# Four of a decode head's six early value loads placed one by one along the round trip of the attention weights, tied to products

## The chip, the cores and the metric

The kernel runs on one core of one Trainium2 chip. Times are microseconds of device time for one execution. Before the change three runs gave 2443.78, 2444.54 and 2450.01; the median is 2444.54.

## The reference

The kernel computes one step of a layer with two kinds of attention heads, for 1024 frames of a new stream (the prompt) and for 16 new frames of each of 8 running streams (the sample, or decode, side), whose keys and values of 1024 earlier frames lie in two caches. Width is 2048, there are 8 stick-breaking heads and 8 retention heads of 128. Cut to what matters here:

```python
def stick_breaking_block(q, k, v, q_start):
    z = jnp.einsum('bqhd,bkhd->bhqk', q, k) * (HEAD_DIM ** -0.5)
    strict = (k_pos[None, :] < q_pos[:, None])[None, None]
    log_beta = jax.nn.log_sigmoid(z)
    log_keep = jnp.where(strict, jax.nn.log_sigmoid(-z), 0.0)
    later = lax.cumsum(log_keep, axis=3, reverse=True) - log_keep
    a = jnp.where(strict, jnp.exp(log_beta + later), 0.0)
    return jnp.einsum('bhqk,bkhd->bqhd', a, v)

    # sample side, in reference()
    q_sb, k_sb, v_sb, gate_sb, q_r, k_r, v_r, gate_r = project(h, w_in[l], pos_s)
    k_all = jnp.concatenate([cache_sb_k[l], k_sb], axis=1)
    v_all = jnp.concatenate([cache_sb_v[l], v_sb], axis=1)
    o_sb = stick_breaking_block(q_sb, k_all, v_all, past)
```

`project` is one multiplication of the normalised input by `w_in` (2048 x 8192); both kinds of heads are normalised, gated, concatenated and multiplied by `w_out`. Everything is float32.

## The kernel before, in words

**Stages.** The prompt's 8 row tiles of 128 and the sample's one tile are worked in two groups: group 0 is tiles 0 to 3 and the sample tile (640 columns), from about 20 to 1270 us of the profile, and group 1 is tiles 4 to 7 (to about 2000 us). In each group a loop runs over the 8 heads, some 140 us each in group 0. The output projection follows. The change touches group 0 alone, because only that group has a decode side.

**The projections, which are most of TensorE's work.** `project` (L226 holds its products) takes a block of 128 columns of `w_in` in four chunks. Each chunk is a load of 256 KB on the SP queue (`wr`, L212), which ScalarE copies to its high part `wh` (L129) and VectorE turns into the rest `wl` (L130); TensorE then does 24 products of it: `wh` with the high and the low part of the input, and `wl` with the high part. `wr`, `wh` and `wl` have four buffers each, so that a load goes out when the chunk four earlier has been split. `project_rows` (L285) does the same for the values of two heads at a time, with the names `wrn`, `whn` and `wln`.

**The attention beside them.** Everything else of a head is written as Python generators, called jobs. After each product (or pair of products) of a projection `tick()` lets at most one job take a step, and the number that a job yields says how many ticks later it wants to go on. So the text order of the program is made by these numbers (`D_ZC`, `D_TO`, `D_TI`, ...), which differ for group 0 and group 1. The tile framework then orders each engine's instructions; `tied(ins)` (L151) tells it, in group 0 only, that `ins` must not come ahead of the last product written so far. This is a matter of order; no semaphore is set or waited for.

**A decode head** (`decode`, from L622), in order of its steps:

- Its cached keys come in 16 loads (`kc`, POOL queue, L642 and after), are transposed by VectorE (`kcT`, L680) and multiplied with the queries (`zc`, L658), eight key loads at a time.
- `load_v(k)` loads 512 KB of cached values (`vc`, L686, SP queue). There are eight such loads. Six of them (`V_BUFS`) are issued in one list comprehension, L692 before the change, as soon as the second half of the keys has been multiplied.
- The scores of the new keys (`zn`) follow, then the weights: sigmoids, masks on POOL, a product scan on VectorE (`weights`).
- **The round trip.** The weights `be` are written to DRAM (`turn_out`, tensor `s_bd`), and 32 ticks later (`D_TO[0]`) read back turned, in four transfers on the SP queue (`turn_in`, L478); another 32 ticks later (`D_TI[0]`) VectorE transposes them in blocks of 32 into `kp`.
- **The products with the values** `pd` (L719), two value loads at a time, 18 ticks apart. As soon as the products with values 0 and 1 are written, values 6 and 7 are loaded; VectorE copies the result (`do`, L726 and L728).

The `kcT` tiles and the `vc` tiles share one set of six buffers. A head uses eight tiles of the one and eight of the other: `vc` 0 and 1 take the buffers of the first half of the keys, `vc` 2 to 5 wait for the products `zc` of the second half, and `vc` 6 and 7 wait for the products `pd` with values 0 and 1.

**Other names that come up.** `kb` is a tile with the weights of the prompt's stick-breaking heads: they too make a round trip through DRAM, but on the POOL queue (its reads are also at L478), are transposed at L575 and multiplied at L615 (`pa`). `ro` and `so` are the outputs of the retention and the stick-breaking heads, which make a round trip of the same kind on the SP queue (L478) for the last normalisation and gating (`sg`, L549). `rs`, `sc`, `pS`, `rkn`, `S` belong to the retention heads. SP also issues the loads `dT` and `st`.

Each engine, and SP as the issuer of its queue, works its own list in order: an instruction that waits holds up what stands behind it in that list.

Of the kernel before, what the change touches and what calls it, by code (L numbers as in the profile page):

```python
# [43 lines left out]
V_BUFS = 6  # L44
D_RET = (9, 5)
D_TO = (32, 23)
D_TA = (14, 0)
D_TB = (17, 33)
D_TI = (32, 13)
# [9 lines left out]
def tile_hybrid_step(  # L59
# [26 lines left out]
    nc = tc.nc  # L86
# [61 lines left out]
    phase = [0]  # L148
    anchor = [None]

    def tied(ins):  # L151

        if phase[0] == 0 and anchor[0] is not None:
            tc.add_manual_dep(
                ins.ins,
                anchor[0].ins.name,
                mybir.DependencyInfo(mybir.DependencyClass.NoSync, mybir.DependencyReason.SCHED_ONLY),
                reason="tied to the products",
            )
# [139 lines left out]
    with ExitStack() as s1:  # L299
# [168 lines left out]
        def turn_out(src, tag, q=nc.scalar):  # L468

            s = scr.tile([src.shape[1], P, P], F32, name=tag)  # L470
            q.dma_start(s.rearrange("k q c -> q k c"), src)
            return s

        def turn_in(s, raw, q):

            for i in range(4):
                tied(
                    q.dma_start(  # L478
                        raw[32 * i : 32 * i + 32, :].rearrange("p (k a) -> p k a", a=32),
                        s[:, :, 32 * i : 32 * i + 32].rearrange("k (j b) a -> b (k j) a", b=32),  # L480
                    )
                )
# [139 lines left out]
        def decode(h, qs, rest):  # L622
# [10 lines left out]
            def chunk(m):  # L633
                s, r = divmod(m, NB)
                j, c = divmod(r, 4)
                return s, j, c
# [14 lines left out]
            for m in range(-KC_AHEAD, 2 * NB + 1):  # L651
                if m > 0 and m % NB == 0:
                    s, _, _ = chunk(m - NB)
# [29 lines left out]
                    loaded.append(load(m + KC_AHEAD))  # L683
            def load_v(k):
                vc = ip.tile([P, NB, P], F32, name="vc", tag="kv", bufs=V_BUFS)
                nc.sync.dma_start(  # L686
                    vc, cache_v[0, :, k * P : (k + 1) * P, h, :].rearrange("b p d -> p b d")
                )
                return vc


            values = [load_v(k) for k in range(V_BUFS)]  # L692
            while "kT" not in rest:
                yield 3
            z = score_tile("zn")
# [3 lines left out]
            yield D_ROW  # L699
            at = kp[:, :n].rearrange("p (k q) -> p k q", q=P)  # L700
            turned = turn_out(be.rearrange("p (k c) -> p k c", c=P), f"s_bd{h}")
            yield D_TO[phase[0]]
            turn_in(turned, be, nc.sync)
            yield D_TI[phase[0]]
            tied(nc.vector.transpose(kp[:, :n], be))
            yield D_TR[phase[0]]
            while "vn" not in rest:
# [5 lines left out]
            for k0 in range(0, 8, 2):  # L713
                yield 2 * D_VC
                for k in (k0, k0 + 1):
                    vc = values.pop(0)
                    for c in range(4):
                        r = slice(32 * c, 32 * c + 32)
                        nc.tensor.matmul(  # L719
                            po[r, : 2 * P], at[:, k, r], vc[:, 2 * c : 2 * c + 2, :], start=(k == 0), stop=(k == 7)  # L720
                        )
                for k in (k0, k0 + 1):
                    if k + V_BUFS < 8:
                        values.append(load_v(k + V_BUFS))
# [161 lines left out]
        for gi, g in enumerate(GROUPS):  # L886
# [7 lines left out]
            for h in range(H):  # L894
# [29 lines left out]
                if SAMPLE in tiles:  # L924
                    drain(sub)
                    sub = Job(decode(h, qs, rest), D_DEC)
# [239 lines left out]
```

## Time and profile before

| | |
|---|---|
| median of three runs | 2444.54 us |
| the profiled execution | 2447.93 us, its span 2446.2 us |
| mean granted TensorE clock of it | 0.982 of full speed |
| TensorE (PE) busy | 2351.9 us, 96% of the span |
| VectorE (DVE) | 1257.4 us, 51% |
| ScalarE (ACT) | 915.6 us, 37% |
| GpSimd (POOL) | 648.2 us, 26% |
| DMA | 418.67 MB, 171 GB/s over the span |
| value loads `vc` | 64 of 512 KB, median 9.5 us from issue to landing |
| weight loads `wr` | 384 of 256 KB, median 4.1 us from issue to landing |

All durations in the text are of the profiled execution. Its page gives the busy time of each engine, the groups of instructions by line (L719 is line 719 of the kernel before), what ended an engine's idle time, and the median time from the issue of a DMA to its landing. `x4` at a row's end means that four like instructions follow one another and are shown as one row. In the lists of waits a row like "PE pa L615 <- DVE kb L575: 31.2, 8, 6.3" reads: TensorE's products `pa` at L615 waited for VectorE's instruction on `kb` at L575, 31.2 us in all, in eight waits, the longest of 6.3. A row of windows has the window's ends and length, the busy time of PE, PEld (weight load into the array), DVE, ACT and POOL with the number of instructions, the granted clock, and the DMA engines' share with GB/s. The lines after L689 are two, four or six higher in the changed kernel: L719 becomes L725, L726 becomes L732, L728 becomes L734.

### The profile page before, as it was taken

How to read it: one execution, taken by the hardware profiler on the slowest of the kernel's cores; microseconds unless marked ns; L12 is line 12 of the kernel's file. 1: busy time of each engine (PE TensorE's matmuls, PEld its weight loads, DVE VectorE, ACT ScalarE, POOL GpSimd, SP SyncE). 2: the span in 40 equal slices, each digit the busy share in tenths (PEclk: the TensorE clock that was granted, in tenths of full speed). 3: DMA queues.
4: the chain of work that ended last, by engine and by line, in shares of the span. 5: the costliest groups of instructions: out<-in, count | busy, mean ns of one | idle time of the engine just before them, and what ended most of it. 6: DMA issues, size and time to landing. Idle time of an engine off the chain costs nothing.

```text
span 2446.2 us, 40473 instructions
## 1 busy us (share of the span) xinstructions
PE 2351.9 (96%) x14832; PEld 2114.5 (86%) x14832; DVE 1257.4 (51%) x2434; ACT 915.6 (37%) x1929; POOL 648.2 (26%) x1029
## 2 busy tenths in 40 slices
PE   7999998999999999999999999999999998999998
PEld 7998898989999898988778888898888876778787
DVE  7245444445455444446555554555555564564544
ACT  6332333333333332333333343333333443444333
POOL 3144353434445243334302111130220221000000
PEclk9999999999999999999999999999999998999999
DMA  7669779696969879698965565566556565676554
GB/s 239 170 129 212 150 175 179 160 203 148 195 151 208 162 170 186 150 214 189 205 157 158 145 144 155 140 156 148 146 148 152 148 169 150 223 220 188 186 182 133
DMA packets 674888, 418.67 MB, mean 171 GB/s; under 512 B 224512, under 2 KB 619776, under 8 KB 672256
## 3 DMA queue, kind: packets, MB, share of 16 engines
q1 hardware_dynamic: 524272, 285.99, 48.2%
q0 software_dynamic: 32256, 71.36, 13.2%
q10 hardware_dynamic: 118160, 58.74, 8.7%
q8 instruction: 116, 1.90, 0.3%
q14 instruction: 84, 0.69, 0.1%
HBM read 336.24 MB, written 79.69 MB: 170 GB/s over the span
## 4 chain that ended last, share of the span: by engine, by line
PE 77%; DMA 12%; DVE 4%; issue 3%; POOL 2%; ACT 2%; ACTq 0%; SPq 0%; DVEq 0%; POOLq 0%
PE acc L226 40%; PE accn L285 16%; PE a L987 4%; PE a L988 4%; PE a L986 3%; DMA mr<-s_y 3%; DMA wr<-w_in 3%; PE pa L615 3%; PE z L585 2%; DMA kb<-s_be 2%; DMA kc<-cache_sb_k 1%; PE pd L719 1%; DMA mr<-s_h 1%; POOL kc L642 1%; PE zc L658 1%
## 5 line engine op out<-in xcount | busy, mean ns | idle before, releaser
L226 PE MATMUL acc<-mh,wh 128*128 128x256 f32 (+2 forms) x2304 | 666.2, 342 | 3.0 <-ACT wh L129 3.0
L226 PE MATMUL acc<-ml,wh 128*128 128x384 f32 (+2 forms) x2304 | 668.2, 343 | 0.0
L226 PE MATMUL acc<-mh,wl 128*128 128x256 f32 (+2 forms) x2304 | 663.3, 341 | 0.1
L130 DVE TENSOR_TENSOR wl<-wr,wh 128x512 fp32r<-128x512 f32 (+1 forms) x576 | 392.7, 687 | 513.2 <-ACT wh L129 505.4
L129 ACT ACTIVATE wh<-wr 128x512 fp32r<-128x512 f32 (+1 forms) x576 | 356.9, 624 | 716.1 <-PE acc L226 317.8
L226 PEld LDWEIGHTS acc<-mh,wh 128*128 128x128 f32 x2304 | 424.3, 190 | 38.8 <-issue 5.8
L226 PEld LDWEIGHTS acc<-mh,wl 128*128 128x128 f32 x2304 | 428.2, 190 | 30.7 <-issue 3.3
L226 PEld LDWEIGHTS acc<-ml,wh 128*128 128x128 f32 x2304 | 426.5, 190 | 32.4 <-issue 4.9
L642 POOL DMA_DIRECT2D kc<-cache_sb_k x512 | 331.5, 653 | 373.6 <-DVE kcT L680 223.2
L285 PE MATMUL accn<-whn,mh 128*128 128x256 f32 x1152 | 330.0, 287 | 1.7 <-DVE rg L312 1.7
L285 PE MATMUL accn<-wln,mh 128*128 128x256 f32 x1152 | 326.7, 284 | 2.1 <-DVE wln L130 2.1
L285 PE MATMUL accn<-whn,ml 128*128 128x256 f32 x1152 | 326.6, 284 | 0.0
L285 PEld LDWEIGHTS accn<-whn,mh 128*128 128x128 f32 x1152 | 221.5, 193 | 11.4 <-issue 7.7
L987 PE MATMUL a<-wl,mh 128*128 128x512 f32 (+1 forms) x576 | 221.1, 384 | 7.6 <-DVE wl L130 7.6
L285 PEld LDWEIGHTS accn<-wln,mh 128*128 128x128 f32 x1152 | 221.8, 193 | 2.7 <-DVE wln L130 2.3
L285 PEld LDWEIGHTS accn<-whn,ml 128*128 128x128 f32 x1152 | 221.8, 193 | 0.0
L988 PE MATMUL a<-wh,ml 128*128 128x512 f32 (+1 forms) x576 | 220.1, 382 | 0.0
L986 PE MATMUL a<-wh,mh 128*128 128x512 f32 (+1 forms) x576 | 219.0, 382 | 0.7 <-DVE so L618 0.5
L130 DVE TENSOR_TENSOR wln<-wrn,whn 128x512 fp32r<-128x512 f32 x128 | 86.9, 686 | 100.3 <-ACT whn L129 100.2
L987 PEld LDWEIGHTS a<-wl,mh 128*128 128x128 f32 x576 | 109.0, 189 | 30.9 <-DVE wl L130 10.2
L129 ACT ACTIVATE whn<-wrn 128x512 fp32r<-128x512 f32 x128 | 79.9, 632 | 132.9 <-PE acc L226 54.4
L503 POOL TENSOR_SCALAR_AFFINE_SELECT kp<-kp 128x128 f32<-128x128 f32 x40 | 14.5, 363 | 429.7 <-ACT kp L497 429.6
(189 smaller groups left out, 2708.8 us busy)
## 6 DMA issues: line engine op xcount, KB each, us to landing
wr<-w_in SPq DMA_DIRECT2D x384, 256.0 KB, 4.1
wr<-w_out SPq DMA_DIRECT2D x184, 256.0 KB, 3.6
wrn<-w_in SPq DMA_DIRECT2D x128, 256.0 KB, 3.3
kc<-cache_sb_k POOLq DMA_DIRECT2D x512, 64.0 KB, 4.9
vc<-cache_sb_v SPq DMA_DIRECT2D x64, 512.0 KB, 9.5
xt<-x_prompt SPq DMA_DIRECT2D x8, 1024.0 KB, 5.8
xr<-x_prompt SPq DMA_DIRECT2D x8, 1024.0 KB, 6.5
out<-out ACTq DMA_DIRECT2D x12, 512.0 KB, 2.8
```

The lines of the kernel that those rows point to most:

```text
L129: nc.scalar.activation(hi, src, AF.Copy)
L130: nc.vector.tensor_tensor(lo, src, hi.bitcast(F32), ALU.subtract)
L226: last = nc.tensor.matmul(a[:, :m], lhs[:, j, :], rhs[w][:, j, o : o + m], start=(w == 0 and j == 0 and n == 0), stop=(w == KT // WQ - 1 a ...
L285: anchor[0] = nc.tensor.matmul(a, lhs[q][:, jj, ts], rhs[:, j, :], start=(w == 0 and j == 0 and n == 0 and t % 2 == 0), stop=(w == KT // 2 ...
L585: nc.tensor.matmul(z[:, :c], q2[a][:, i * P : (i + 1) * P], k2[b][:, s : s + c], start=(m == 0), stop=(m == 2),)
L615: nc.tensor.matmul(po[:, :P], at[:, j, :], vn[:, j, :], start=(j == 0), stop=(j == t))
L642: nc.gpsimd.dma_start(kc[32 * i : 32 * i + 32, :].rearrange("p (k d) -> p k d", d=32), cache_k[0, 2 * c + j, s * 512 : (s + 1) * 512, h, 3 ...
L658: mm = nc.tensor.matmul(z[r, :], qp[:, j, r], ready[2 * j + c // 2][:, c % 2, :], start=(j == 0), stop=(j == 1),)
L719: nc.tensor.matmul(po[r, : 2 * P], at[:, k, r], vc[:, 2 * c : 2 * c + 2, :], start=(k == 0), stop=(k == 7))
L986: nc.tensor.matmul(a[:, :width], hi[q][:, j, ts], wh, start=(k == 0), stop=False)
L987: nc.tensor.matmul(a[:, :width], hi[q][:, j, ts], wl, start=False, stop=False)
L988: nc.tensor.matmul(a[:, :width], lo[q][:, j, ts], wh, start=False, stop=(k == KT - 1))
```

## The change

`decode` issues the first two value loads where all six were issued. Loads 2 and 3 go into the pause between writing the weights `be` out and reading them back, one at its start and one 16 ticks later; loads 4 and 5 go into the pause between reading back and transposing, likewise. These four are passed to `tied`, so that the framework does not move them ahead of the products written before them. Loads 6 and 7 stay where they were. The number of instructions, the buffers and the transfers are the same.

```diff
             def load_v(k):
                 vc = ip.tile([P, NB, P], F32, name="vc", tag="kv", bufs=V_BUFS)
-                nc.sync.dma_start(
+                ld = nc.sync.dma_start(
                     vc, cache_v[0, :, k * P : (k + 1) * P, h, :].rearrange("b p d -> p b d")
                 )
+                if 2 <= k < V_BUFS:
+                    tied(ld)
                 return vc
 
 
-            values = [load_v(k) for k in range(V_BUFS)]
+            values = [load_v(k) for k in range(2)]
             while "kT" not in rest:
                 yield 3
...
             turned = turn_out(be.rearrange("p (k c) -> p k c", c=P), f"s_bd{h}")
-            yield D_TO[phase[0]]
+            for _ in range(2):
+                values.append(load_v(len(values)))
+                yield D_TO[phase[0]] // 2
             turn_in(turned, be, nc.sync)
-            yield D_TI[phase[0]]
+            for _ in range(V_BUFS - 4):
+                values.append(load_v(len(values)))
+                yield D_TI[phase[0]] // 2
             tied(nc.vector.transpose(kp[:, :n], be))
```

Since the program's text order and the framework decide each engine's list together, the lists show more than the diff. First SP's list in head 5, from the head's first value loads on. `vc` are value loads, `wr` weight chunks, `be` the four reads of the turned weights; before:

```order
L686 DMA vc<-cache_sb_v 128x8x128 x2
L212 DMA wr<-w_in 128x4x128 x2
L686 DMA vc<-cache_sb_v 128x8x128 x4
L212 DMA wr<-w_in 128x4x128 x4
L478 DMA be<-s_bd_10460 32x36x32 x4
L212 DMA wr<-w_in 128x4x128 x5
L686 DMA vc<-cache_sb_v 128x8x128 x2
L478 DMA ro<-s_rk_6_10693 32x20x32 x4
L478 DMA so<-s_o_5_4_0_10719 32x16x32 x4
L212 DMA wr<-w_in 128x4x128 x2
```

And after the change:

```order
L686 DMA vc<-cache_sb_v 128x8x128 x2
L212 DMA wr<-w_in 128x4x128 x4
L686 DMA vc<-cache_sb_v 128x8x128
L212 DMA wr<-w_in 128x4x128
L686 DMA vc<-cache_sb_v 128x8x128
L212 DMA wr<-w_in 128x4x128 x2
L478 DMA be<-s_bd_10452 32x36x32 x4
L686 DMA vc<-cache_sb_v 128x8x128 x2
L212 DMA wr<-w_in 128x4x128 x2
L686 DMA vc<-cache_sb_v 128x8x128 x2
L478 DMA ro<-s_rk_6_10693 32x20x32 x4
L478 DMA so<-s_o_5_4_0_10719 32x16x32 x4
```

Of the weight loads, two more now stand between the first two value loads and the third; between `be` and values 6 and 7, where five stood, there are two, behind values 4 and 5; the other three follow behind the reads of `ro` and `so`, ahead of the two that stood there.

Second, VectorE's list in head 5 from the copy of the decode result (`do`) on; before:

```order
L726 COPY do<-pd 128x128
L492 MEMSET kp 128x1
L728 SCALAR_TENSOR_TENSOR do<-pd,dec,do 128x128
L747 TENSOR_TENSOR sc<-rs,dT 128x128
L548 STREAM_TRANSPOSE kT<-so 128x512
L728 SCALAR_TENSOR_TENSOR do<-pd,dec,do 128x128
L549 SCALAR_TENSOR_TENSOR sg<-kT,gains,sg 128x512
L766 COPY ro<-pa 128x128
L137 TENSOR_SCALAR ov<-ssq_9457 128x1
L130 TENSOR_TENSOR wl<-wr,wh 128x512
```

And after:

```order
L732 COPY do<-pd 128x128
L492 MEMSET kp 128x1
L734 SCALAR_TENSOR_TENSOR do<-pd,dec,do 128x128
L753 TENSOR_TENSOR sc<-rs,dT 128x128
L548 STREAM_TRANSPOSE kT<-so 128x512
L734 SCALAR_TENSOR_TENSOR do<-pd,dec,do 128x128
L549 SCALAR_TENSOR_TENSOR sg<-kT,gains,sg 128x512
L772 COPY ro<-pa 128x128
L137 TENSOR_SCALAR ov<-ssq_9457 128x1
L130 TENSOR_TENSOR wl<-wr,wh 128x512
L787 COPY S<-pS 128x128
L130 TENSOR_TENSOR wl<-wr,wh 128x512
```

Three `wl` that stood ahead of the first of these rows now stand behind them: the `wl` shown is that of an earlier chunk than the one shown before.

Third, TensorE's list in head 5 behind the last products with values; before, a chunk's products with `wh` come in pairs of the high and the low part of the input (`mh`, `ml`) and are followed by those with `wl`:

```order
L226 MATMUL acc_10844<-mh_147,wh 128x256
L226 MATMUL acc_10845<-mh_147,wh 128x384
L226 MATMUL acc_10844<-ml_148,wh 128x256
L226 MATMUL acc_10845<-ml_148,wh 128x384
L226 MATMUL acc_10844<-mh_147,wl 128x256
L226 MATMUL acc_10845<-mh_147,wl 128x384
```

And after:

```order
L784 MATMUL pS<-rv,rkn 128x128
L751 MATMUL rs<-rq,rk 128x128
L226 MATMUL acc_10844<-mh_147,wh 128x256
L226 MATMUL acc_10845<-mh_147,wh 128x384
L226 MATMUL acc_10844<-ml_148,wh 128x256
L226 MATMUL acc_10845<-ml_148,wh 128x384
L769 MATMUL pa<-rv,sc 128x128
L226 MATMUL acc_11037<-mh_141,wh 128x256
L226 MATMUL acc_11038<-mh_141,wh 128x384
L226 MATMUL acc_11037<-ml_142,wh 128x256
L226 MATMUL acc_11038<-ml_142,wh 128x384
L226 MATMUL acc_10844<-mh_147,wl 128x256
```

Products that need only `wh`, four of them of the next projection (`acc_11037`, `acc_11038`), now stand ahead of the first one that needs `wl`.

## The prediction

> **What bounds the kernel now.** I read the page first, then TensorE's waits.
>
> ```profile
> span 2446.2 us, 40473 instructions
> PE 2351.9 (96%) x14832; PEld 2114.5 (86%) x14832; DVE 1257.4 (51%) x2434; ACT 915.6 (37%) x1929; POOL 648.2 (26%) x1029
> PE pa L615 <- DVE kb L575: 31.2, 8, 6.3
> ```
>
> TensorE is busy for 96% of the span, so a gain can only come from its idle time (2446.2 - 2351.9 = 94 us) and from time at a low clock. The third row is its longest wait: the attention products of L615 wait for VectorE's transpose of `kb` (L575), eight times, 31.2 us in all. I then looked for where these waits lie, in windows of two microseconds, and cut two windows round the one large gap of each of heads 1 to 6 of the first group: the gap itself, and the 7 us behind it (columns: window, its length, then busy time of PE, PEld, DVE, ACT, POOL, then granted clock, DMA share, GB/s).
>
> ```profile
> 380.00:386.20 6.20, 0.02 (x1) 0.02 (x1) 2.29 (x6) 2.42 (x6) 0.09 (x1) 0.66 1.13 141
> 522.80:526.20 3.40, 0.44 (x4) 0.18 (x2) 2.32 (x7) 1.68 (x5) 0.00 (x0) 0.88 1.24 153
> 660.90:664.90 4.00, 0.07 (x1) 0.00 (x0) 2.22 (x5) 1.66 (x4) 0.00 (x0) 1.00 1.01 138
> 801.00:805.40 4.40, 0.47 (x4) 0.20 (x2) 2.37 (x7) 2.31 (x6) 0.00 (x0) 0.99 1.09 141
> 940.80:944.80 4.00, 0.05 (x2) 0.00 (x1) 2.13 (x5) 1.28 (x4) 0.00 (x0) 1.00 1.04 156
> 1081.10:1085.20 4.10, 0.25 (x2) 0.00 (x0) 2.75 (x7) 1.79 (x5) 0.00 (x0) 1.00 1.18 144
> 386.20:393.20 7.00, 7.00 (x31) 7.00 (x32) 3.57 (x11) 3.49 (x7) 0.00 (x0) 0.57 0.76 191
> 526.20:533.20 7.00, 7.00 (x31) 7.00 (x32) 3.91 (x14) 3.49 (x7) 0.00 (x0) 0.57 0.83 208
> 664.90:671.90 7.00, 6.98 (x39) 6.98 (x40) 4.12 (x11) 4.88 (x10) 0.00 (x0) 0.76 0.70 161
> 806.00:813.00 7.00, 6.95 (x30) 6.95 (x31) 3.91 (x14) 3.49 (x7) 0.00 (x0) 0.56 0.76 198
> 944.80:951.80 7.00, 7.00 (x39) 7.00 (x40) 4.16 (x12) 4.52 (x10) 0.00 (x0) 0.76 0.79 184
> 1085.40:1092.40 7.00, 7.00 (x39) 7.00 (x40) 3.94 (x14) 3.50 (x7) 0.00 (x0) 0.77 0.84 207
> ```
>
> Length less PE busy gives the idle time: 6.18, 2.96, 3.93, 3.93, 3.95 and 3.85, together 24.8 us. Behind each gap TensorE works at a mean clock of 0.56 to 0.77; the missing shares are 0.43 + 0.43 + 0.24 + 0.44 + 0.24 + 0.23 = 2.01, times 7 us = 14.1 us. These six places cost 38.9 us.
>
> What a gap waits for is told by the chain of waits (head 5, 915 to 950 us) and by the SP queue there (start, duration, operation).
>
> ```profile
> 928.42 14.05 DMA wr<-w_in
> 942.56 0.64 ACT wh L129
> 944.11 0.64 DVE kb L575
> 944.80 1.71 PE pa L615 x8
> ```
>
> ```profile
> 909.02 3.48 SPq L212 DMA_DIRECT2D wr<-w_in  x2
> 916.89 8.07 SPq L686 DMA_DIRECT2D vc<-cache_sb_v  x4
> 925.06 11.07 SPq L212 DMA_DIRECT2D wr<-w_in  x4
> 937.17 8.43 SPq L478 DMA_DIRECT2D be<-s_bd  x4
> ...
> 968.24 2.05 SPq L212 DMA_DIRECT2D wr<-w_in  x2
> ```
>
> SP stands from 912.5 to 916.9, then puts out four value loads of 512 KB in a row; a weight load issued behind them takes 14.05 us to land. ScalarE's and VectorE's lists are in order: `wh` and `wl` of that chunk stand ahead of the `kb` transpose, and TensorE's next products behind it.
>
> **The change part by part.** No instruction is added or removed, and the `tied` call adds no wait on the chip; it only fixes the order.
>
> (1) *The burst goes.* Of the four weight loads behind the burst of head 5 the first now stands ahead of all moved value loads, the second behind one (8.07 / 4 = 2.0 us of issue), the last two behind two; heads 2, 3, 4 and 6 read the same. The load that landed at 942.5 is the second. SP reaches it at 928.4, when its buffer comes free, in either order; with nothing but one value load ahead I expect it to land between the run's median and today's value in this stretch:
>
> ```profile
> wr<-w_in SPq DMA_DIRECT2D x6, 256.0 KB, 9.9
> vc<-cache_sb_v SPq DMA_DIRECT2D x2, 512.0 KB, 15.4
> wr<-w_in SPq DMA_DIRECT2D x384, 256.0 KB, 4.1
> ```
>
> That is 928.4 + 4.1 to 9.9, so 932.5 to 938.3, and 1.3 us for the two splits ahead of `kb`: in time for TensorE's stop at 940.8. So these five gaps go, with the low clock behind them. In head 1 both loads that the `kb` transpose needs stay behind value loads, the second behind two, so 4 us earlier than today against a gap of 6.2; and its read of `kb` on the POOL queue, hidden behind the weights today, is late next:
>
> ```profile
> 372.80 0.65 POOL L478 DMA_DIRECT2D kb<-s_be  x1 [1.98 <-issue]
> kb<-s_be POOLq DMA_DIRECT2D x4, 64.0 KB, 7.2
> ```
>
> 372.8 + 7.2 + the transpose's 0.7 = 380.7, against a stop at 380.0. So head 1 keeps about 2 us (bounds 0 and the whole gap of 6.2). Together -38.9 + 2.
>
> A rule of the Trainium skill bears on the clock: the page TensorE: Matmul & The Clock Gate (What's actually happening) has the array fall to half clock after an idle window of about 3.4 us. The second gap, 2.96 us, is shorter, and 0.57 was granted behind it; the trace does not agree there. By the rule the 3.0 us of low clock behind that gap would have another cause and stay, and the sum would be -28 us; I go by the rows.
>
> (2) *Three weight loads per head move behind the last pair.* SP's list now has value loads 4 and 5 behind the `be` reads, then two weight loads, then loads 6 and 7, which wait for the products that free their buffers (`pd`, k = 0 and 1), and only then the other three weight loads, behind eight small reads. The pair's position is reached at:
>
> ```profile
> 955.32 1.07 PE L719 MATMUL pd<-vc,kp 128*32 128x256 f32 x16
> 956.40:977.00 20.60, 17.61 (x112) 16.36 (x113) 1.00 0.95 184
> wr<-w_in SPq DMA_DIRECT2D x2, 256.0 KB, 6.0
> 975.54 0.29 DVE L726 COPY do<-pd 128x128 f32<-128x128 f32 x1 [1.80 <-PE pd L719]
> 978.20 0.68 DVE L130 TENSOR_TENSOR wl<-wr,wh 128x512 fp32r<-128x512 f32 x1
> ```
>
> Counted in the two lists, 4.6 chunks of 24 products are loaded beyond this point now (7.6 before), 110 products. The second row counts L226 alone: 112 of them run in the 20.6 us from 956.4, so the first moved chunk is needed at 977. Its load goes out where today's first one behind the small reads does, 968.24, lands 6.0 us later (third row) at 974.2 and is split by ScalarE in 0.64: 974.9. That is 2 us of slack. Its `wl` is now listed behind the copies of `do` and the gating, in the place of the `wl` at 978.20, which ends at 978.88; TensorE's new list puts eight products that use only `wh` first (8 x 17.61 / 112 = 1.3 us, and three small ones), so it asks for `wl` at 978.6. I charge +1 us per head, 6 in all, since several such orderings meet here. Bounds: 0 if they fit, and 7 us per head if the load is 4 us late (the same load took 9.9 among the burst) with 3 us of low clock behind, as in the second gap.
>
> (3) *Heads 0 and 7.* In head 0 three of the four loads still stand in a row: 0. Head 7 has two gaps:
>
> ```profile
> 1220.42 1.16 PE L615 MATMUL pa<-vn,kb 128*128 128x128 f32 x8 [3.36 <-DVE kb L575]
> 1253.62 0.50 PE L226 MATMUL acc<-mh,wh 128*128 128x512 f32 x1 [2.49 <-ACT wh L129]
> ```
>
> The first follows its burst, now halved; the second is short of weights, and the weights loaded ahead of the last pair fall from 2.9 to 2.3 chunks (0.6 x 3.8 us = 2.3 us more). Taken as 0, with -5 and +5 as bounds.
>
> (4) *The values land later.*
>
> ```profile
> 967.70 1.07 PE L719 MATMUL pd<-vc,kp 128*32 128x256 f32 x16
>   PEld pd L719: 0.2, 1
> ```
>
> Value loads 4 and 5 now follow `be`, by today's times at 945.6 (937.17 + 8.43). Their products come at 967.7 (first row), 22 us later, against the 15.4 us of a load in today's burst; TensorE waits 0.2 us in all for a value today (second row). Nothing.
>
> Sum: -38.9 + 2 + 6 + 0 = -31 us. The profiled execution took 2447.93 us, 1.7 more than its span and 3.4 above the median of the runs; 2444.5 - 31 = **2414 us** (rounded up from 2413.6).
>
> **The rivals.** (a) *The gaps were partly POOL's.* If the reads of `kb` are as late as the weights in half of the heads (for it: head 1's row above; against it: the chain goes by `wr` in head 5), heads 1, 2 and 6 keep 6.2 + 3.0 + 3.9 of idle and 3.0 + 3.0 + 1.6 of clock, 20.7 us in place of the 2: 2432 us.
>
> (b) *The other side: starved behind the last pair.* The three moved weight loads wait on SP behind loads whose release comes from TensorE itself. For it: 2 us of slack only, head 7's gap of 2.49 with few weights ahead. Against it: SP's queue is emptier at that point, since these three loads are not in flight. At 7 us per head it takes back 42 of the 38.9: 2444.5 - 36.9 + 42 + 5 (head 7) = 2455 us. It decides from 36.9 / 6 = 6.2 us per head; at half the price it gives 2444.5 - 36.9 + 21 = 2429 us.
>
> (c) *Values late.* If `pd` has to wait 5 us for values 4 and 5 in six heads, 30 us come back: 2444 us. Against it: the 22 us of (4). The Trainium skill, DMA: Bandwidth & Descriptors (Rules for kernel authors), advises to issue a transfer early and wait late, which speaks against this change in just this way; the trace, where early issue cost six gaps, does not agree with it for a shared queue.
>
> (d) *No effect*, because the small reads and key loads, not the values, fill the DMA engines (share above 1 in every gap): 2444 us.
>
> **How the numbers follow.** The forecast has 0.64, (a) 0.14, (b) at full price 0.07 and at half price 0.05, (c) 0.05, (d) 0.05. The range goes from 2400 (no new cost and head 7 gaining 5: 38.9 + 5 = 44 less) to 2438, which holds (a) and the cheaper (b) and leaves out 0.17. A change within 0.3% (7.3 us) is not told from none: faster are the forecast, (a) and the cheaper (b), 0.83; same (c) and (d), 0.10; slower 0.07.
>
> **What would show it.** Right: TensorE's waits lose most of the 31.2 us on `kb`; the clock stays near 1.00 in the places above; weight loads land in under 8 us there; the distance from one head's value loads to the next shrinks by 5 to 6 us. Wrong: a wait for `wh` or `wl` of more than 2 us behind each last pair (b), a wait for `vc` (c), or the gaps still there with `kb` released by DMA (a).

## The result, and the profile after

| | before | after |
|---|---|---|
| median of four runs | 2444.16 us | 2414.38 us |
| lowest and highest | 2441.84 to 2450.01 | 2410.33 to 2417.12 |
| the profiled execution, and its span | 2447.93, 2446.2 | 2413.81, 2412.1 |

The ratio is 0.9865 with a 95% interval of 0.985 to 0.9879: 1.35% faster, 33 us by the ratio and 30 by the medians. The profiled executions differ by 34.1, since the one before lay 3.8 us above the median of its four. The page's first lines and TensorE's waits after the change:

```profile
span 2412.1 us, 40463 instructions
PE 2338.0 (97%) x14832; PEld 2099.1 (87%) x14832; DVE 1255.4 (52%) x2434; ACT 913.6 (38%) x1929; POOL 647.9 (27%) x1029
PE zc L658 <- DVE kcT L680: 5.5, 3, 2.2
PE pa L615 <- DVE kb L575: 4.7, 5, 2.3
PE acc L226 <- ACT wh L129: 4.7, 2, 4.2
```

The wait of `pa` for `kb`, 31.2 us in the kernel before, is down to 4.7. To see where the time came from I cut both traces at the copy of the decode queries (`qs`), of which each head has one: head 0, heads 1 to 6 together, and the rest of the program. Before, then after (columns: window, length, busy time of PE, PEld, DVE, ACT, POOL, granted clock, DMA share, GB/s):

```profile
131.80:283.50 151.70, 143.32 (x1032) 132.96 (x1031) 72.96 (x162) 46.47 (x109) 61.70 (x104) 0.95 0.77 168
283.50:1104.60 821.10, 795.14 (x5888) 749.34 (x5887) 403.29 (x846) 272.64 (x589) 336.91 (x561) 0.98 0.82 176
1104.60:2446.20 1341.60, 1297.27 (x7073) 1117.41 (x7071) 713.25 (x1272) 531.32 (x1125) 214.70 (x312) 0.99 0.63 166
```

```profile
131.80:279.60 147.80, 141.02 (x1032) 131.53 (x1032) 72.98 (x162) 46.37 (x109) 61.35 (x104) 0.98 0.79 171
279.60:1068.70 789.10, 784.57 (x5884) 736.46 (x5883) 400.71 (x845) 270.22 (x588) 335.48 (x560) 1.00 0.84 182
681.80:818.90 137.10, 134.44 (x1005) 125.32 (x1004) 68.19 (x146) 46.31 (x102) 56.00 (x94) 1.00 0.83 183
1068.70:2412.10 1343.40, 1296.78 (x7077) 1117.03 (x7075) 713.89 (x1273) 532.15 (x1126) 215.88 (x313) 0.99 0.63 166
```

Heads 1 to 6 are 32.0 us shorter (821.1 to 789.1), head 0 is 3.9 shorter, the rest (head 7 and all that follows) 1.8 longer. In heads 1 to 6 TensorE's idle time (length less PE busy) falls from 25.96 to 4.53, which is 21.4 us, and its busy time by 10.6: the same products at a granted clock of 1.00 instead of 0.98. Over half of the idle time that is left lies in head 4 (the third row after: 137.10 - 134.44 = 2.66).

The mechanism shows in ScalarE's copies of weight chunks in head 5 (start, duration, then in brackets the idle time before and what ended it), before the change and then after it; 933.80 and 904.15 stand at the same place of the sequence:

```profile
933.80 0.64 ACT L129 ACTIVATE wh<-wr 128x512 fp32r<-128x512 f32 x1
940.05 0.63 ACT L129 ACTIVATE wh<-wr 128x512 fp32r<-128x512 f32 x1 [5.61 <-DMA wr<-w_in]
942.56 0.63 ACT L129 ACTIVATE wh<-wr 128x512 fp32r<-128x512 f32 x1 [1.87 <-DMA wr<-w_in]
```

```profile
904.15 0.64 ACT L129 ACTIVATE wh<-wr 128x512 fp32r<-128x512 f32 x1
906.83 0.63 ACT L129 ACTIVATE wh<-wr 128x512 fp32r<-128x512 f32 x1 [2.05 <-PE acc L226]
910.35 0.63 ACT L129 ACTIVATE wh<-wr 128x512 fp32r<-128x512 f32 x1 [2.89 <-PE acc L226]
```

Before, ScalarE waits for weight loads to land. After, the weights are there, and it waits for TensorE to give a `wh` buffer back: the weights run ahead of the products again.

### The profile page after: what moved, and what is told of

It reads as the page before. It is cut to its first block, busy times and chain, and to the rows that moved or that the text cites. A ratio compares the mean times of both kernels' runs of the same rounds, so it can differ in the third digit from the quotient of the medians.

```text
span 2412.1 us, 40463 instructions
## 1 busy us (share of the span) xinstructions
PE 2338.0 (97%) x14832; PEld 2099.1 (87%) x14832; DVE 1255.4 (52%) x2434; ACT 913.6 (38%) x1929; POOL 647.9 (27%) x1029
## 3 DMA queue, kind: packets, MB, share of 16 engines
q0 software_dynamic: 32256, 71.36, 13.5%
## 4 chain that ended last, share of the span: by engine, by line
PE 84%; DMA 8%; DVE 4%; ACT 1%; issue 1%; POOL 1%; SPq 0%; DVEq 0%; ACTq 0%; POOLq 0%
PE acc L226 45%; PE accn L285 17%; PE a L993 3%; PE a L994 3%; PE a L992 3%; DMA mr<-s_y 3%; PE pa L615 3%; PE z L585 2%; DMA wr<-w_in 2%; PE zc L658 1%; PE pd L725 1%; DMA wr<-w_out 1%; DVE ml L130 1%; DVE out L1054 1%; DVE wl L130 1%
## 5 line engine op out<-in xcount | busy, mean ns | idle before, releaser
L226 PE MATMUL acc<-mh,wh 128*128 128x256 f32 (+2 forms) x2304 | 664.0, 341 | 6.4 <-ACT wh L129 4.7
L226 PE MATMUL acc<-ml,wh 128*128 128x384 f32 (+2 forms) x2304 | 665.4, 342 | 0.0
L226 PE MATMUL acc<-mh,wl 128*128 128x256 f32 (+2 forms) x2304 | 659.2, 339 | 0.9 <-DVE wl L130 0.7
L226 PEld LDWEIGHTS acc<-mh,wh 128*128 128x128 f32 x2304 | 420.8, 189 | 41.9 <-ACT wh L129 5.6
L226 PEld LDWEIGHTS acc<-ml,wh 128*128 128x128 f32 x2304 | 422.6, 189 | 33.4 <-issue 6.2
L226 PEld LDWEIGHTS acc<-mh,wl 128*128 128x128 f32 x2304 | 424.2, 189 | 31.0 <-DVE wl L130 2.6
L993 PEld LDWEIGHTS a<-wl,mh 128*128 128x128 f32 x576 | 109.4, 190 | 29.8 <-DVE wl L130 9.0
L478 POOL DMA_DIRECT2D be<-s_be x128 | 94.1, 741 | 131.0 <-DMA s_be<-be 116.5
```

What stands on the lines that cost most here:

```text
L226: last = nc.tensor.matmul(a[:, :m], lhs[:, j, :], rhs[w][:, j, o : o + m], start=(w == 0 and j == 0 and n == 0), stop=(w == KT // WQ - 1 a ...
L478: q.dma_start(raw[32 * i : 32 * i + 32, :].rearrange("p (k a) -> p k a", a=32), s[:, :, 32 * i : 32 * i + 32].rearrange("k (j b) a -> b (k ...
L993: nc.tensor.matmul(a[:, :width], hi[q][:, j, ts], wl, start=False, stop=False)
```

## The experiments

Every kernel was timed in three rounds beside the kernel before, in three groups of four; the median before was 2445.95, 2444.33 and 2447.06 us in these. "Idle" is TensorE's idle time in heads 1 to 6 of the profiled execution, cut as above.

| kernel | us | ratio, 95% interval | idle, us | length of heads 1 to 6, us |
|---|---|---|---|---|
| before (profile above) | | | 26.0 | 821.1 |
| the change | 2414.38 | 0.9865, 0.985 to 0.9879 | 4.5 | 789.1 |
| burst halved | 2417.16 | 0.9883, 0.9855 to 0.9912 | 3.6 | 788.5 |
| four spread in the first pause | 2443.97 | 0.9984, 0.9966 to 1.0002 | 19.2 | 809.0 |
| four in a row, later | 2442.77 | 0.9984, 0.9968 to 1.0 | 28.0 | 821.2 |
| before, an eighth of the bytes | 2397.74 | 0.9804, 0.9779 to 0.983 | 1.6 | 784.2 |
| before, half of the bytes | 2397.99 | 0.9811, 0.9791 to 0.9831 | 1.8 | 784.9 |
| before, three quarters | 2407.30 | 0.9854, 0.9838 to 0.9871 | 2.2 | 784.3 |
| four in a row on ScalarE's queue | 2436.61 | 0.9969, 0.9954 to 0.9984 | 13.5 | 800.0 |
| the change, an eighth of the bytes | 2397.80 | 0.9805, 0.9786 to 0.9824 | 1.8 | 783.5 |
| the change, all eight loads an eighth | 2383.83 | 0.9757, 0.9739 to 0.9774 | 1.6 | 785.0 |
| last pair apart too | 2405.55 | 0.9840, 0.9815 to 0.9864 | 0.6 | 783.6 |
| first loads late in head 0 | 2414.04 | 0.9869, 0.9851 to 0.9886 | 3.2 | 786.0 |
| the same in heads 0 and 7 | 2414.07 | 0.9866, 0.9846 to 0.9886 | 2.9 | 785.8 |

The theory at the start: a weight load that stands on SP's queue behind value loads lands late by the bytes ahead of it, and holds up ScalarE's and VectorE's lists and then TensorE's products. The rivals: any row of loads costs a gap, SP's standing costs it, the other engines' changed lists bring the gain, or the loads' bytes hit weights on any queue.

**Half of the burst.** Loads 2 and 3 stay in a row where the burst stood; only 4 and 5 move.

```diff
-            values = [load_v(k) for k in range(2)]
+            values = [load_v(k) for k in range(4)]
...
-            for _ in range(2):
-                values.append(load_v(len(values)))
-                yield D_TO[phase[0]] // 2
+            yield D_TO[phase[0]]
```

> Value loads 2 and 3 stay in a row where the burst of four stood (1 MB instead of 2 MB); 4 and 5 go behind the reads of be, as in the change. All lists but SP's are those of the changed kernel. Queue theory (a weight load behind the burst lands late because the burst is ahead of it on SP's queue): the weight load that landed at 942.6 in head 5 of the kernel before lands 4 us earlier (half of the burst's 8.07 us), so gaps of 3 to 4 us shrink to nothing and that of head 1 to about 2: 2418 us, TensorE's waits of pa for kb below 8 us. Rival (four loads must stand apart; any burst costs a gap): half of the gaps' 32 us stay, 2430 us.

Measured: 2417.16, and of the wait for `kb` this is left:

```profile
PE pa L615 <- DVE kb L575: 4.7, 6, 2.3
```

The whole gain of heads 1 to 6 is there, so two loads in a row cost no gap. Setting loads 2 and 3 apart, half of the change's text, is worth nothing that these runs can tell.

**All four spread in the first pause.**

```diff
-            for _ in range(2):
+            for _ in range(4):
                 values.append(load_v(len(values)))
-                yield D_TO[phase[0]] // 2
+                yield D_TO[phase[0]] // 4
...
-            for _ in range(V_BUFS - 4):
-                values.append(load_v(len(values)))
-                yield D_TI[phase[0]] // 2
+            yield D_TI[phase[0]]
```

> All four value loads are placed in the first pause (8 ticks apart, tied), none behind the reads of be. In SP's list of head 5 this is three weight loads, one value load, one weight load, three value loads, one weight load, then be; five weight loads stay ahead of the last pair, as before the change, and the other engines' lists are those of before but for a few places. Queue theory: the second weight load, on which the gap depends, has one value load ahead of it instead of four, so the gaps of heads 1 to 6 go: 2412 us if moving three weight loads behind the last pair costs the changed kernel 2 to 6 us, 2414 to 2418 if it costs nothing (the fourth weight load lands behind three value loads, 6 us of issue). Rival (the gain comes from the moved weight loads and the changed lists of VectorE and TensorE, not from the burst): 2440 us or more.

Measured: 2443.97, and the interval of its ratio reaches 1.0002: hardly any of the gain. Expectation and theory fell here. The profiled execution was the fastest of ten (2436.31); even in it 19.2 us of idle time are left in heads 1 to 6, which are 12.1 us shorter than before. TensorE's waits and the window of heads 1 to 6; then SP's queue in head 5; then pieces of the chain of waits there (start, duration, what):

```profile
PE pa L615 <- DVE kb L575: 18.7, 6, 4.3
PE pd L715 <- DVE kp L709: 8.5, 3, 3.5
284.94:1093.92 808.98, 789.80 (x5888) 742.50 (x5887) 403.31 (x846) 272.09 (x588) 337.18 (x561) 0.99 0.81 178
```

```profile
908.01 0.58 SPq L686 DMA_DIRECT2D vc<-cache_sb_v  x1
914.34 0.37 SPq L212 DMA_DIRECT2D wr<-w_in  x1
914.76 6.15 SPq L686 DMA_DIRECT2D vc<-cache_sb_v  x3
921.08 3.04 SPq L212 DMA_DIRECT2D wr<-w_in  x1
928.55 5.91 SPq L478 DMA_DIRECT2D be<-s_bd  x4
```

```profile
921.08 12.93 DMA wr<-w_in
934.12 0.64 ACT wh L129
941.96 1.38 DVE kp L709
943.48 0.46 PE pd L715 x2
```

The weight load behind the first single value load no longer decides; the next one does, behind the other three: 12.93 us to land. Its copy stands ahead of other work of ScalarE and VectorE, up to the transpose of the decode weights (L709), on which `pd` waits. In the change only two value loads, not four, stand ahead of the last weight loads before `be`.

The landing time alone does not decide, though. With the burst halved, the first weight load behind the two value loads of head 5 went out at 893.86 and took 13.7 us, longer than the 12.93 here. ScalarE's copy of it there, and then the copy of the late load here:

```profile
907.91 0.63 ACT L129 ACTIVATE wh<-wr 128x512 fp32r<-128x512 f32 x1 [2.05 <-PE acc L226]
```

```profile
934.12 0.63 ACT L129 ACTIVATE wh<-wr 128x512 fp32r<-128x512 f32 x1 [5.25 <-DMA wr<-w_in]
```

There ScalarE waited for TensorE, and the load was in time: it was asked for 14.0 us after its issue. Here ScalarE had nothing else to do from 7.8 us after the issue on (934.12 - 5.25 - 921.08). So at the later place in the list the weights have less in hand, and a row of three value loads there brings the wait back.

**All four in a row, one weight load later.** As above, without the pauses between the four. SP's list then differs from that of the kernel before in one thing, one more weight load ahead of the burst; the other lists are those of before.

```diff
-            for _ in range(2):
-                values.append(load_v(len(values)))
-                yield D_TO[phase[0]] // 2
+            for _ in range(4):
+                values.append(load_v(len(values)))
+            yield D_TO[phase[0]]
...
-            for _ in range(V_BUFS - 4):
-                values.append(load_v(len(values)))
-                yield D_TI[phase[0]] // 2
+            yield D_TI[phase[0]]
```

> All four value loads in a row at the place where the change puts load 2. SP's list differs from that of the kernel before in one thing: one more weight load stands ahead of the burst (three instead of two); all other lists are those of before. Queue theory: the weight load that sets the gap is the second behind the old burst, so it still stands behind 2 MB: gaps stay at two thirds or more, 2436 us (2430 to 2446). Rival (it is enough that the burst leaves the place where SP stands for the buffers): 2415 us.

Measured: 2442.77, the gaps are all there ("PE pa L615 <- DVE kb L575" 31.3 us), as the theory had it. Leaving the place where SP stood for the buffers is of no use by itself.

**The bytes alone.** The kernel before, with loads 2 to 5 cut to 1, 4 or 6 of their 8 blocks; all lists stay as they were, and so does SP's wait for the buffers (4.4 us ahead of the row in head 5 before, 4.2 with an eighth). The products read the loaded blocks in place of the others (not shown).

```diff
+                nb = 1 if 2 <= k < V_BUFS else NB
                 nc.sync.dma_start(
-                    vc, cache_v[0, :, k * P : (k + 1) * P, h, :].rearrange("b p d -> p b d")
+                    vc[:, :nb, :], cache_v[0, :nb, k * P : (k + 1) * P, h, :].rearrange("b p d -> p b d")
                 )
```

> The kernel before, with value loads 2 to 5 cut to an eighth of their bytes (64 KB; the products use that eighth for all the streams, so the values of these four blocks are partly left out). Every list is that of the kernel before, and SP stands as long for the buffers' release. Queue theory, the bytes ahead of the weight load decide: the gaps of heads 1 to 6 go, waits of pa for kb under 8 us, 2410 us. Rival, SP's standing (4.4 us before the burst) delays the weight loads: gaps stay at over half, 2428 us or more. Rival, key loads and small reads fill the DMA engines: 2444 us.

> The kernel before with value loads 2 to 5 cut to half their bytes (256 KB each, 1 MB in a row; the products use the first quarter of the streams for all, so part of the values is left out). All lists are those of the kernel before. Bytes theory (a weight load lands late by the bytes put out ahead of it in a short time): the weight load that landed at 14 us lands at 9 to 10, the gaps of heads 1 to 6 go: 2410 us (2402 to 2418). Rival (the changed kernel and the one with the burst halved won by their other lists, with loads 4 and 5 behind be; four loads in a row keep the gap whatever their size above an eighth): 2430 us or more.

> The same with three quarters of the bytes (384 KB each, 1.5 MB in a row). Bytes theory: landing at about 12 us, gaps of 1 to 2.5 us in place of 3 to 6 and some low clock: 2428 us (2420 to 2436). Rival (threshold at three loads' bytes, as with three in a row): 2440 us.

Measured: 2397.74, 2397.99 and 2407.30. What TensorE still waits for `kb` in the whole program with three quarters of the bytes (1.3 of it in heads 1 to 6), and SP's four value loads of head 5 with an eighth and with three quarters:

```profile
PE pa L615 <- DVE kb L575: 7.4, 5, 3.4
884.10 1.81 SPq L687 DMA_DIRECT2D vc<-cache_sb_v  x4
889.45 5.25 SPq L687 DMA_DIRECT2D vc<-cache_sb_v  x4
```

The gaps are a matter of bytes: with the lists of before and SP standing as long, the gaps of heads 1 to 6 are gone. That ends the rival on SP's standing, and the one by which the other engines' changed lists bring the gain.

The bytes act in two ways, and the theory had only one of them. A weight load behind the row lands late; but SP is also held longer while it issues the row (8.07 us with whole loads), so that the weight load goes out late. The first weight load behind the row of head 5, whose buffer is free when VectorE has split the chunk four earlier:

| bytes of loads 2 to 5 | went out after its buffer was free, us | landed after its issue, us | ScalarE waited for it, us |
|---|---|---|---|
| 0.25 MB | 2.3 | 4.6 | 0 |
| 1 MB | 2.7 | 9.7 | 0 |
| 1.5 MB | 5.7 | 10.7 | 0.35 |
| 2 MB (before) | 8.6 | 14.9 | 5.61 |

The sizes were off: all three kernels came out below what I had expected (2410, 2410 and 2428). At 1.5 MB idle time in heads 1 to 6 is 2.2 us, at 2 MB it is 26.0. The table tells why so little shows up to 1.5 MB: the delay grows all along, what the weights have in hand covers it up to some length, and only what exceeds it shows. At 1.5 MB the load came just in time. Between 1.5 and 2 MB nothing was measured. Half and three quarters differ by 9.3 us in the medians but by only 5.6 in the profiled executions, and none of that lies in heads 1 to 6 (784.9 and 784.3); where the rest lies is not shown.

**The same row on ScalarE's queue.**

```diff
-                ld = nc.sync.dma_start(
+                ld = (nc.scalar if 2 <= k < V_BUFS else nc.sync).dma_start(
...
```

(with the four in a row at the place of load 2; in ScalarE's list two of them then stand ahead of the write of `be` and two behind it, as the rows below show.)

> Value loads 2 to 5 in a row at the place of the change's load 2, but issued by ScalarE on its own queue; no weight load stands behind them on SP's queue. ScalarE issues four DMAs more per head (4 times 0.5 to 1 us) and the lists shift somewhat. Queue-order theory (only loads behind the values on the same queue are late): waits of pa for kb below 10 us, 2418 us (2410 to 2426). Rival (the bytes fill the 16 DMA engines that all queues share, so weight loads are late on any queue): gaps as with the late burst on SP, 2440 us.

Measured: 2436.61, between the two theories and nearer to the rival's 2440, for a reason of its own. ScalarE in head 5, then TensorE's waits in the whole program:

```profile
913.66 1.06 ACTq L686 DMA_DIRECT2D vc<-cache_sb_v  x2
917.50 0.37 ACTq L471 DMA_DIRECT2D s_bd<-be  x1
917.91 11.48 ACTq L686 DMA_DIRECT2D vc<-cache_sb_v  x2
929.43 0.31 ACT L535 ACTIVATE sq<-so 128x128 f32<-128x128 f32 x1 [15.16 <-DMA vc<-cache_sb_v]
930.64 1.67 ACT L129 ACTIVATE wh<-wr 128x512 fp32r<-128x512 f32 x3
```

```profile
PE acc L226 <- ACT wh L129: 19.4, 8, 6.3
PE pa L615 <- DVE kb L575: 9.4, 3, 5.0
```

Issuing the last two loads held ScalarE's list for 11.48 us; three chunks of weights had landed meanwhile and were copied in one go at 930.64. In heads 1 to 6, 12.6 of TensorE's 13.5 us of idle time are waits for `wh` and 0.6 for `kb`. Heads 1 to 6 are 21.1 us shorter than before, but head 0 is 8.2 longer (159.9 us). The weight load that SP issued at 916.2, while the row was on ScalarE's queue, took this long to land (the three values are one load's):

```profile
L212 SPq DMA_DIRECT2D wr<-w_in x1: 368/368/368, 916.2 to 916.2; - x1
DMA to landing us min/median/max: 11.1/11.1/11.1
```

The longest landing of a weight load in the stretch ahead of `be` (60 us from a head's `qs` to the first read of `be`) was 11.1 to 12.9 us over heads 1 to 6, against 13.4 to 17.2 with the row on SP and 9.0 to 11.1 with the change. So the rival holds in part: the row delays weight loads from another queue too. The load issued at 916.2 had no other load under way on SP's queue and still took 11.1 us, where the run's median is 4.0. That it took less than with the row on SP does not show that a queue of its own helps, for only two of the four value loads were out when it was issued. What cost the time in heads 1 to 6 is neither theory's: the queue's engine is held while it issues, and with it all that stands behind. The Trainium skill, DMA: Bandwidth & Descriptors (Issuing engines are not separate DMA queues), says that transfers of all issuers share the engines and that several issuers save only issue time, usually small beside the transfer. The first agrees with the 11.1 us; the second does not agree with the 11.48, for the slowest of this kernel's value loads took 17.4 us to land.

**What the moved weight loads cost.** The changed kernel with the same cut to an eighth in loads 2 to 5:

> The changed kernel with value loads 2 to 5 cut to an eighth (64 KB; the products use that eighth for all streams, so part of the values is left out). Against the kernel before with the same cut (2397.7 us) this leaves only the changed lists: three weight loads behind the last pair and the shifted places on VectorE and TensorE. Prediction's part (2) as written: +6 us in heads 1 to 6, 2404. If the moved weight loads cost nothing: 2398 (2395 to 2401). If the changed lists are themselves of use: below 2393.

Measured: 2397.80, against 2397.74 for the kernel before with that cut. The three weight loads per head that stand behind the last pair, and the shifted places on VectorE and TensorE, cost nothing that can be measured in heads 1 to 6 (783.5 and 784.2 us); but there loads 2 to 5 are small, and the queue is emptier than in the changed kernel. In the profiled executions the part behind head 6 is 5.5 us longer (1340.0 against 1334.5) and head 0 3.1 shorter.

**What value loads still cost after the change.** All eight cut to an eighth:

> The changed kernel with all eight value loads cut to an eighth (64 KB; the products use it for all streams, so most values are left out). Bound on what value loads still cost after the change. With the eighth in loads 2 to 5 alone the kernel before came to 2397.7. If the change left nothing in heads 1 to 6, only heads 0 and 7 can gain: 2396 us (2390 to 2404). Rival, the values still cost idle time in heads 1 to 6: below 2388.

Measured: 2383.83. This is below the expected range, where the rival lay, but not for the rival's reason: heads 1 to 6 are no shorter than with loads 2 to 5 cut (785.0 and 783.5 us). Most of what is left is in head 0 (136.4 us, 147.8 with whole loads) and behind head 6 (1329.2 against 1343.4).

**Two tries at what is left.** In head 0, and then in heads 0 and 7, loads 0 to 3 all in the first pause:

```diff
-                if 2 <= k < V_BUFS:
+                if (0 if late else 2) <= k < V_BUFS:
...
-            values = [load_v(k) for k in range(2)]
+            late = h == 0
+            values = [] if late else [load_v(k) for k in range(2)]
...
-            for _ in range(2):
+            for _ in range(4 if late else 2):
                 values.append(load_v(len(values)))
-                yield D_TO[phase[0]] // 2
+                yield D_TO[phase[0]] // (4 if late else 2)
```

> The changed kernel, but in head 0 values 0 and 1 are not issued ahead of the scores: loads 0 to 3 go into the first pause, 8 ticks apart, 4 and 5 as in the change. With all value loads cut to an eighth head 0 was 11 us shorter (136.4 against 147.7), so the bytes of values 0 and 1, put out while the second half of the keys is loaded, are what is left to gain there: 2406 us (2402 to 2412). Rival (head 0 is bound by key loads whatever the values do): 2414.

> The same placing in head 0 and in head 7. Head 7 after the change still waits 4.2 us for a weight load behind the last pair, which this does not move; its two first values leave the place ahead of six weight loads. Bytes theory: head 0 as in the run with head 0 alone, head 7 between 3 us gained and 3 lost (values 0 to 5 now stand closer together): 2406 us (2402 to 2412). Rival (the six loads in a short stretch make a new gap in head 7, as four loads did before): 2414 or more.

Measured: 2414.04 and 2414.07, no gain, against 2406 expected for both; head 0 took 151.7 and 151.0 us. That its loads cost time is shown by the run with all loads cut; that issuing the first two later helps did not come true.

And the last pair set apart:

```diff
-                if 2 <= k < V_BUFS:
+                if 2 <= k:
...
-                yield 2 * D_VC
+                yield D_VC
+                if k0 == 2:
+                    values.append(load_v(7))
+                yield D_VC
...
-                for k in (k0, k0 + 1):
-                    if k + V_BUFS < 8:
-                        values.append(load_v(k + V_BUFS))
+                if k0 == 0:
+                    values.append(load_v(6))
```

> The changed kernel with the last pair placed apart too: value load 6 where it was, load 7 nine ticks later, both tied. In heads 1 to 6 one weight load stands between them, in head 7 the earlier loads alternate with weight loads. Bytes theory: in heads 1 to 6 nothing is left to gain, in head 7 up to 5 us: 2412 us (2406 to 2417). Rival (load 7 comes too late for its products): a wait for values of over 1 us per head, 2420 us.

Measured: 2405.55 (2403.09 to 2409.88), half a microsecond below the expected range. On the same chip the two kernels with the first loads late took 2409.45 to 2415.04, and the change on its own chip 2410.33 to 2417.12. It is the fastest kernel here that loads everything, though its interval against before still overlaps that of the change.

Heads 1 to 6 have 0.56 us of idle time left, 4 less than with the change, and behind head 6 it is 3.7 us shorter (2402.4 - 1062.7 = 1339.7). The first was not expected, and no run shows its cause.

## Why the prediction was right, and where its steps were not

The time came out at 2414.38 where 2414 was predicted; the terms did not. From the profiled executions, except for the third row, which is from the two kernels with cut loads (in the changed kernel such a cost would be contained in the first two rows):

| step | predicted, us | measured, us |
|---|---|---|
| gaps of heads 1 to 6 | -24.8, +2 kept in head 1 | -21.4 of idle |
| low clock behind them | -14.1 | -10.6 of busy time |
| three weight loads behind the last pair | +6 | 0 |
| head 0; head 7 and all behind it | 0 | -3.9 and +1.8 |
| sum | -31 | -34.1 |

**(1) The burst goes: right in its effect, wrong in part of its reason.** All six gaps went, head 1's too (0.64 us of idle in the whole head, where 2 were kept for `kb`). Of the idle time that is left, 2.66 us are head 4's, mostly a wait of `zc` for VectorE's `kcT` (2.2 us). VectorE had stood for a read of `kb` on POOL's queue, which is ahead of `kcT` in its list:

```profile
754.10 0.45 DVE L575 STREAM_TRANSPOSE kb<-kb 128x256 f32<-128x256 f32 x1 [4.38 <-DMA kb<-s_be]
756.36 0.70 DVE L680 STREAM_TRANSPOSE kcT<-kc 128x512 f32<-128x512 f32 x1
```

Two steps of the reason failed. The first is "SP reaches it at 928.4, when its buffer comes free, in either order". The split that frees this buffer, before the change; then the same split after it, and the load:

```profile
922.59 0.66 DVE L130 TENSOR_TENSOR wl<-wr,wh 128x512 fp32r<-128x512 f32 x1
```

```profile
897.29 0.66 DVE L130 TENSOR_TENSOR wl<-wr,wh 128x512 fp32r<-128x512 f32 x1
897.98 0.37 SPq L212 DMA_DIRECT2D wr<-w_in  x1
```

Before, the buffer was free at 923.25 and SP came 5.2 us later, held by the value loads and the weight load ahead. After, the load went out at once and landed in 7.6 us, within the 4.1 to 9.9 expected. So it came 11.6 us earlier, 5.1 by its issue and 6.5 by its landing. That every weight load in these places would land in under 8 us did not hold: the slowest of each head took 9.0 to 11.1, without a gap.

The second is "with nothing but one value load ahead": that a weight load decides by the value loads directly ahead of it, so that setting them apart cures the gap. With one ahead of the second weight load the gap came back at the next one. What cured it is that two of the four loads went behind the reads of `be`: 1 MB less in that stretch, whether or not the other two were set apart.

**The low clock was mis-sized.** I took the missing share of the clock as lost time. Two windows of equal length behind the gap of head 1 in the kernel before, at a granted clock of 0.50 and then of 1.00:

```profile
388.30:391.90 3.60, 3.60 (x15) 3.60 (x15) 2.10 (x7) 1.34 (x5) 0.00 (x0) 0.50 0.66 187
392.60:396.20 3.60, 3.60 (x26) 3.60 (x26) 2.89 (x8) 1.13 (x3) 0.00 (x0) 1.00 0.52 145
```

A window counts 15 products at half clock and 26 at full clock, not half as many. Products overlap (at half clock one of 128x256 takes 415 ns and one of 128x384 522, yet such a pair starts every 533), so their pace is told by their starts: from one 128x256 product of L226 over a 128x384 product to the next it is 0.533 us at 0.50 (median of 39 in this trace) and 0.293 us at 1.00 (median of 2045), 1.82 times as long. A microsecond at half clock thus loses 1 - 0.293 / 0.533 = 0.45, not 0.5, and the 28.2 us at half clock (14.1 / 0.5) lose 12.7. The busy time of heads 1 to 6 fell by 11.7 to 13.4 in the five kernels with cut loads, and by 10.6 with the change. The 2.1 us between 12.7 and 10.6 are not explained.

The rule by which the second gap, 2.96 us long, could not have caused the low clock behind it (the Trainium skill, TensorE: Matmul & The Clock Gate, What's actually happening) fails here once more: without the gap that low clock is gone too, the clock of heads 1 to 6 being 1.00.

**(2) The charge of 6 us was unnecessary.** The comparison of the two kernels with cut loads gives 0.06 us in the medians. TensorE's waits in heads 1 to 6 after the change (279.6 to 1068.7 us), the two longest and the one for weights, show that the 2 us of slack held:

```profile
PE zc L658 <- DVE kcT L680: 2.2, 1, 2.2
PE pa L769 <- DVE ov L137: 1.0, 3, 0.6
...
PE acc L226 <- DVE wl L130: 0.3, 2, 0.2
```

Only head 7 shows rival (b), as (3) had it (the chain of waits there after the change):

```profile
1208.86 9.60 DMA wr<-w_in
1218.48 0.64 ACT wh L129
1219.16 1.22 PE acc L226 x2
```

The wait there grew from 2.49 to 4.2 us, 1.7 of the 2.3 worked out, while the wait for `kb` fell from 3.36 to 1.8. Head 0's 3.9 us were not foreseen; it took 148.6 to 153.1 us in the other kernels with whole loads on SP's queue, so a part of them may be spread between executions.

**(4) Values late: right.** TensorE's waits for `vc` rose from 0.2 to 1.0 us. Of the rivals, (a), (c) and (d) did not come.

So the terms that were measured do not add up to the forecast's -30.9. 6 us were charged for nothing; 3.5 were too much on the clock and 1.4 of idle time were not won (-22.8 against -21.4); heads 0 and 7 gave 2.1 more: -30.9 - 6 + 3.5 + 1.4 - 2.1 = -34.1, the difference of the profiled pair. The medians differ by 29.8, and the ratio's interval allows 30 to 37. That the time met the forecast within half a microsecond is luck: errors of several microseconds in the terms cancelled, and the spread between executions is as large as what was left of them.

What stays open: whether four value loads ahead of `be`, strictly one between two weight loads, would do. The list put three of them in a row, and no kernel here has the even one. How much the bytes and how much the place in the list count was not separated for the later places: 1.5 MB in a row at the place of before left 2.2 us of idle time, three loads of the same 1.5 MB at the later place, behind one more, 19.2.

## What to carry to other kernels

When loads for later use share a queue with loads that feed the next products, count the bytes that go out ahead of the weight loads while these have something in hand: here 1.5 MB at one place of the list was hidden and 2 MB cost 26 us of idle time, while two loads in a row did as well as two set apart. Count both the late landing and the late issue, for the issuing engine is held too. The same 2 MB, one load apart and three in a row later, left most of the idle time. Move a part of the bytes past the stretch where the reserve is thin, and test that with the bytes cut and every list unchanged, since an order table moves much else. A forecast that meets the time can still have its terms wrong; the windows by stage showed it.

## What the runs showed of the hardware that was not expected

- At a granted clock of 0.50 a pair of the projection's float32 products (128x256 and 128x384) took 1.82 times as long as at 1.00 (one pair every 0.533 us against 0.293), not twice.
- Issuing a DMA can hold the issuing engine's list for long, and here the hold grew with the bytes: four value loads took SP 8.07 us to issue at 512 KB each, 5.25 at 384 KB and 1.81 at 64 KB. On ScalarE's queue two loads of 512 KB took 11.48 us, two others issued 4 us earlier 1.06.
- A weight load with no other load under way on its own queue took 11.1 us to land while value loads were under way on ScalarE's queue, against a median of 4.0 in that run.
